# First stage in another order: modulation first, all of v among the filters

## The chip, the cores and the metric

The kernel runs on one core of a Trainium2 chip. The metric is the device time of one execution in microseconds (us). Each execution does the whole step in one launch. The engines of the core are TensorE (PE, with its weight loads PEld), VectorE (DVE), ScalarE (ACT), GpSimd (POOL) and SyncE (SP), which here only issues transfers. Each engine works through its own list of instructions in order and waits where an operand or a buffer is not ready.

## The reference

One inference step of a layer with D = 1024 on T = 640 tokens: 128 of a prompt and 512 of a sample, with separate conditioning vectors (c_ctx and c). Cut to what matters here:

```python
mod = (silu(cond) @ ada_w + ada_b).reshape(6, 1024)      # shift1 scale1 gate1 shift2 scale2 gate2
h = x * (1 + scale1) + shift1
q, f_fwd, f_bwd, i_raw, g_raw, hy, mg = split(h @ w_in)   # w_in: 1024 x 10240
# filters: three sine layers of 64, then @ filt_w4, times a window; to the frequency domain
# HGRN2 mixer: gates from f, v = i_raw, chunkwise scan per head and direction
# Hyena mixer: short conv, long conv through the frequency domain with the filters
mix = (sigmoid(mga) * (o_a @ proj_a) + sigmoid(mgb) * (o_b @ proj_b)) @ w_out
x = layer_norm(ALPHA * x + gate1 * mix)
x = layer_norm(ALPHA * x + gate2 * ((silu(gt) * up) @ ffn_w_out))   # gt, up from h2 @ ffn_w_in
```

Outputs are both token groups and the final scan states of the prompt.

## The kernel before, in words

All products are fp32. A product is made as three passes of rounded parts: high by high, high by low, low by high. The transposed input is held as hTh and hTl, four tiles each of 128 x 2 x 640. Each weight tile (512 KB, named raw) is loaded by SP, cast to its high part wh by ACT (L357 before) and its low part wl is made by a subtraction, on DVE or POOL (L181 is the helper tt that records all such operations). A table HIE says which engine casts, WSUB which one subtracts for the first units, LOOK how far ahead a unit's weights are asked for.

The program's stages: a first stage (function start), Winograd products M1 of several column groups of w_in, the long convolution, proj_b, the HGRN heads, w_out, the FFN and the output. The first stage runs over the tokens of the table PLAN:

- x0..x4 load the five token blocks, T0..T4 transpose them on PE into xT; p, t, q load and transpose small parameters; mlp is the filter MLP with its three sine layers.
- k0..k2 load the cosine/sine table and split it (kth, ktl).
- L0..L3 load a quarter of the filters' last weight (w4) and its window (win); A0..A3 make the windowed filter (matmuls ks; the results af, abh, abl), B0..B3 transform it (matmuls kp and k, 54 of 256 columns; sums and differences go to tiles ko); W0..W3 store ko to DRAM (kd) by the queue of ACT.
- D0..D3 load two 1 MB halves each of a block of ada_w into a ring of three buffers (tag araw), M0..M3 multiply them with the conditioning vectors (matmuls ada), copy the result (md), transpose it (adaT) and add it up into modT.
- h0..h7 scale and shift one eighth of xT with modT and split it into hTh and hTl.
- V0, V1 make a quarter of v each: two weight tiles, 120 matmuls of 256 columns, copies by ACT (L709), one store to vd by SP (L710). Before, the other two quarters are the tokens v2 and v3 of HGSEQ, the table of the HGRN stage, between g0/e0 and a1.
- e0 and e2 make the operands of the Winograd products (mb, then m5, m7, m6, m4, high and low) on DVE and ACT from hTh and hTl. The first of them closes the pool se, in whose memory the ring araw lies, and puts its tiles there. g, w and the digits load and split weights of M1 and run its products (L668). Q and Z are later blocks of ada_w, whose halves go through a buffer of tag v.

The tokens set the priority of the instructions; a scheduler then gives each engine its list, and the pools of buffers decide what must wait for what. In HGSEQ, a and b are the projections f of a head in both directions, q and g those of q and g, e the elementwise work of a head (Ln, scans, exponentials, products t), s its scan matmuls, that begin with transpositions kT.

```python
v = (vp if p < 2 else hg["p"]).tile([P, NB, 256], F32, tag="v", bufs=1 + p // 2, name=f"v{p}")
ada_load(*divmod(i, 2), vp, "v", 1)          # ada_next: the later ada blocks
close_se(); mo["y"], mo["close_t"] = pool("mtp")   # first call of m1_operands
```

Of the kernel before, what the change touches and what calls it, by code (L numbers as in the profile page):

```python
# [1784 lines left out]
```

## Time and profile before

| | |
|---|---|
| median of 3 runs | 1434.0 us (1432.09 to 1435.02) |
| profiled execution | 1434.2 us, its span 1431.9 us |
| PE busy | 1381.0 us, 96% of the span |
| DVE, ACT, POOL busy | 992.3, 617.3, 64.1 us |
| DMA | 195.64 MB, mean 137 GB/s |

The span reaches from the first to the last instruction. A matmul's record is longer than the distance to the next one, because matmuls overlap; what a matmul costs is read from the distance of their starts. A row of the waits says which instruction waited, for which, how long in all, how often and how long at most. A wait for several things is put down to the one that came last.

### The profile page before, as it was taken

To read this page: it belongs to the slowest core of one execution; us is meant where nothing else is said; L and a number is where in the kernel's file an instruction comes from. 1 tells how busy PE (TensorE), PEld (TensorE's weight loads), DVE (VectorE), ACT (ScalarE), POOL (GpSimd) and SP (SyncE) were. 2 spreads that over 40 slices of the span, in tenths; PEclk is the share of its full clock that TensorE was granted. 3 is DMA by queue.
4 is the path that set the end of the run, shared out by engine and by line. 5 is a ranking of instruction groups with operands and counts; after the bars stand their busy time and mean duration, and the time that the engine had idled before them with its cause. 6 is when DMAs were issued, how large, how long until landed. Compare 5 with 4: busy or idle time off the path is not lost. (4 is left out here: it accounts for less than half of the span.)

```text
span 1431.9 us, 23453 instructions
## 1 busy us (share of the span) xinstructions
PE 1381.0 (96%) x9513; PEld 1293.4 (90%) x9513; DVE 992.3 (69%) x1751; ACT 617.3 (43%) x1011; POOL 64.1 (4%) x56
## 2 busy tenths in 40 slices
PE   4999999999999999999999999999999999999997
PEld 2689889999999989999999999988999898898886
DVE  6886786647889734568788875579976665756426
ACT  3555554433323212455665673337543443442121
POOL 4230000020000000000000000000000000000003
PEclk9999999999999999999999999999999999999999
DMA  7944665674333374422232224632343323357211
GB/s 247 324 141 141 217 216 175 208 244 154 90 100 102 105 230 151 145 74 86 70 95 63 67 67 148 224 103 84 111 119 100 113 82 116 91 182 272 74 60 74
DMA packets 198856, 195.64 MB, mean 137 GB/s; under 512 B 7581, under 2 KB 155773, under 8 KB 197980
## 3 DMA queue, kind: packets, MB, share of 16 engines
q1 hardware_dynamic: 194860, 179.75, 39.9%
q0 software_dynamic: 2160, 9.15, 1.7%
q10 hardware_dynamic: 1728, 5.24, 0.9%
q8 instruction: 74, 1.21, 0.4%
q14 instruction: 34, 0.28, 0.1%
HBM read 162.91 MB, written 31.21 MB: 136 GB/s over the span
## 5 line engine op out<-in xcount | busy, mean ns | idle before, releaser
L181 DVE TENSOR_TENSOR wl<-raw,wh 128x1024 fp32r<-128x1024 f32 x96 | 117.3, 1224 | 134.8 <-ACT wh L357 131.2
L357 ACT CAST wh<-raw 128x1024 fp32r<-128x1024 f32 x90 | 94.1, 1049 | 221.8 <-PE pb L611 41.0
L1423 PE MATMUL fo<-wh,act 128*128 128x512 f32 (+1 forms) x440 | 130.7, 380 | 0.0
L1423 PEld LDWEIGHTS fo<-wh,act 128*128 128x128 f32 x440 | 81.2, 188 | 15.9
L1423 PE MATMUL fo<-wl,act 128*128 128x512 f32 (+1 forms) x220 | 83.4, 379 | 0.0
L611 PE MATMUL hy<-hTh,wh 128*128 128x320 f32 x256 | 79.6, 311 | 0.0
L611 PE MATMUL hy<-hTh,wl 128*128 128x320 f32 x256 | 79.2, 309 | 0.0
L611 PE MATMUL hy<-hTl,wh 128*128 128x320 f32 x256 | 79.1, 309 | 0.0
L611 PE MATMUL f<-hTh,wh 128*128 128x320 f32 x224 | 70.7, 316 | 0.0
L611 PE MATMUL f<-hTl,wh 128*128 128x320 f32 x224 | 69.7, 311 | 0.0
L611 PE MATMUL f<-hTh,wl 128*128 128x320 f32 x224 | 69.2, 309 | 0.0
L181 POOL TENSOR_TENSOR y<-y,gb 128x512 f32<-128x512 f32 x8 | 11.6, 1454 | 908.8 <-ACT y L170 908.5
L1423 PEld LDWEIGHTS fo<-wl,act 128*128 128x128 f32 x220 | 41.3, 188 | 7.9
L611 PEld LDWEIGHTS hy<-hTh,wh 128*128 128x128 f32 x256 | 48.1, 188 | 0.0
L611 PEld LDWEIGHTS hy<-hTl,wh 128*128 128x128 f32 x256 | 48.1, 188 | 0.0
L611 PEld LDWEIGHTS hy<-hTh,wl 128*128 128x128 f32 x256 | 48.1, 188 | 0.0
L707 PE MATMUL v<-wl,hTh 128*128 128x256 f32 x160 | 45.4, 287 | 1.6 <-DVE wl L181 1.6
L170 ACT ACT_TABLE_LOAD x36 | 46.2, 1283 | 1.4 <-PEq L1769 0.7
L707 PE MATMUL v<-wh,hTl 128*128 128x256 f32 x160 | 45.4, 286 | 0.1
L707 PE MATMUL v<-wh,hTh 128*128 128x256 f32 x160 | 45.1, 286 | 0.0
L611 PEld LDWEIGHTS f<-hTl,wh 128*128 128x128 f32 x224 | 42.2, 188 | 0.0
L611 PEld LDWEIGHTS f<-hTh,wh 128*128 128x128 f32 x224 | 42.1, 188 | 0.0
(2291 smaller groups left out, 4708.1 us busy)
## 6 DMA issues: line engine op xcount, KB each, us to landing
raw<-in_w_in SPq DMA_DIRECT2D x52, 512.0 KB, 4.0
rf<-in_ffn_w_in SPq DMA_DIRECT2D x42, 512.0 KB, 4.3
araw<-in_ada_w SPq DMA_DIRECT2D x20, 1024.0 KB, 5.8
rm<-in_w_in SPq DMA_DIRECT2D x28, 512.0 KB, 4.8
raw<-in_ffn_w_out SPq DMA_DIRECT2D x22, 512.0 KB, 5.0
sd<-my SPq DMA_DIRECT2D x28, 320.0 KB, 2.3
kk<-kd SPq DMA_DIRECT2D x20, 256.0 KB, 2.7
ad<-y SPq DMA_DIRECT2D x16, 320.0 KB, 4.4
```

The costliest lines, as they stand in the source:

```text
L170: r = S.activation(out, in_, func, bias=bias, scale=scale)
L181: return (eng or V).tensor_tensor(out=out, in0=a, in1=b, op=op)
L357: (V.tensor_copy if HIE[i] == "V" else S.copy)(hi, raw)
L611: r = PE.matmul(ps[:, 0:HT], w[a][:, k, :], x[b][:, k, c0:c0 + HT], start=k == 0 and i == 0, stop=k == kt - 1 and i == 2)
L707: PE.matmul(ps[:, (t - t0) * 256:(t - t0) * 256 + 256], hT[b][:, k, t * P:t * P + P], w[a][:, k % 4, :], start=k == 0 and i == 0, stop=k = ...
L1423: PE.matmul(ps, x(t, b, k0 + kk), w[a][:, kk, :], start=first and kk == 0 and i == 0, stop=last and kk == nk - 1 and i == 2)
```

## The change

PLAN is in another order. The loads of ada_w, of x and the modulation M0 to M3 and all of h come ahead of the second filter; then the filters and the four quarters of v alternate: L1 B0 V0 A1 W0 L2 B1 V1 A2 W1 L3 B2 V2 A3 W2 q B3 e0 g0 W3 V3. A new token c transposes the two conditioning vectors from a tile of their own (crow), which two DMAs of ACT's queue load, and makes their sigmoid ahead of the MLP; before, they were part of prow2 and of token t. v2 and v3 leave HGSEQ, and all four quarters use one buffer. The results ko of a filter leave from the ring araw (and kop from the ring xs of the pool se), before from buffers of the weight stream or from a tile of their own. All scaling of h goes to ACT (HMOD), all splits of the first stage's weights to DVE (WSUB).

```diff
-PLAN = """x0 k0 L0 k1 x4 k2 p mlp t L1 T0 x3 T4 A0 x2 D0 T2 A1 x1 L2 B0 M0 T1 D2 A2 M2 T3 h0 L3 B1 D1 A3 h1 B2 M1 D3 h2 h3 M3 h4 W2 W0 h5 h6 h7 W1 q V0 e0 B3 g0 W3 V1 m w0 e2 10 20 g1 ...
-HMOD = "SVSSVSSS"
+PLAN = """c mlp p x0 L0 x1 D0 x2 t k0 T0 T1 k1 D2 T2 x3 x4 k2 M0 D1 A0 T3 T4 M2 D3 M1 M3 h0 h1 h2 h3 h4 h5 h6 h7 L1 B0 V0 A1 W0 L2 B1 V1 A2 W1 L3 B2 V2 A3 W2 q B3 e0 g0 W3 V3 m w0 e2 10 20 g1 ...
+HMOD = "SSSSSSSS"
-WSUB = "VGGVVGGG"
+WSUB = "VVVVVVVVVVVV"
-HGSEQ = """a0 b0 q0 g0 e0 v2 v3 a1 b1 ...
+HGSEQ = """a0 b0 q0 g0 e0 a1 b1 ...
...
+    crow = sp.tile([16, P], F32, name="crow")
+    S.dma_start(crow[0:8], I["c_ctx"].rearrange("(k p) -> k p", p=P))
+    S.dma_start(crow[8:16], I["c"].rearrange("o (k p) -> (o k) p", p=P))
...
+    def cond_T():
+        ps = tr_bank("pr2_ps")
+        PE.transpose(ps[:, 0:16], crow, ident[0:16, 0:16])
+        V.tensor_copy(cT.rearrange("p a k -> p (a k)"), ps[:, 0:16])
         act(csig, cT, AF.Sigmoid)
...
-            if cc < 2:
-                t = wp.tile([P, n, 2, 256], F32, tag=("wh", "wl")[cc], bufs=HL_BUFS, name=f"ko{cc}_{nm}")
-            else:
-                t = sp.tile([P, n, 2, 256], F32, tag="ko", bufs=1, name=f"ko{cc}_{nm}")
+        ko = se.tile([P, 2, 2, 2, 256], F32, tag="araw", bufs=3, name=f"ko{cc}")
...
-        t = kout(1, "p")
+        t = se.tile([P, 1, 2, 256], F32, tag="xs", bufs=3, name=f"kop{cc}")
...
-            v = (vp if p < 2 else hg["p"]).tile([P, NB, 256], F32, tag="v", bufs=1 + p // 2, name=f"v{p}")
+            v = vp.tile([P, NB, 256], F32, tag="v", bufs=1, name=f"v{p}")
...
-        stream["stop"] = 4
+        stream["stop"] = 8
```

HIE and LOOK get four entries more at their head (S and 2), for the four weight tiles that V2 and V3 add to the first stage.

Three places show how instructions move. First SP's queue in the first stage, before (araw are halves of ada_w, w and win a filter's loads, raw the weights of V0 and V1):

```order
L397 DMA araw_0_318<-in_ada_w 128x4x512
L397 DMA araw_1_320<-in_ada_w 128x4x512
L450 DMA xs_393<-in_x_sample 128x1024
L523 DMA w_2_395<-in_filt_w 64x2x256 x2
L526 DMA win_398<-in_win 128x5x256
L397 DMA araw_0_505<-in_ada_w 128x4x512
L397 DMA araw_1_507<-in_ada_w 128x4x512
L523 DMA w_3_606<-in_filt_w 64x2x256 x2
L526 DMA win_609<-in_win 128x5x256
L397 DMA araw_0_682<-in_ada_w 128x4x512
...
L349 DMA raw_917<-in_w_in 128x4x256
```

The same queue after the change:

```order
L402 DMA araw_0_257<-in_ada_w 128x4x512
L402 DMA araw_1_259<-in_ada_w 128x4x512
L455 DMA xs_275<-in_x_sample 128x1024
L455 DMA xs_277<-in_x_sample 128x1024
L520 DMA kt_279<-in_kt 128x768
L402 DMA araw_0_303<-in_ada_w 128x4x512
L402 DMA araw_1_305<-in_ada_w 128x4x512
L402 DMA araw_0_412<-in_ada_w 128x4x512
L402 DMA araw_1_414<-in_ada_w 128x4x512
L528 DMA w_1_496<-in_filt_w 64x2x256 x2
L531 DMA win_499<-in_win 128x5x256
L354 DMA raw_571<-in_w_in 128x4x256
```

All eight halves of ada_w now stand ahead of the second filter's loads and of the first weight of v.

Second, DVE where the operands of M1 are made. Before, they begin ahead of the third filter's last sums (ko_1_815) and run on between the sums of the fourth (ko_0_1132):

```order
L181 TENSOR_TENSOR mb_0_1077<-hTh_872,hTl_873 128x640
L181 TENSOR_TENSOR ko_1_815<-k_1_1_788,ev_1_813 128x512
...
L181 TENSOR_TENSOR mb_0_1078<-mb_0_1078,mb_0_1075 128x640
L181 TENSOR_TENSOR m5l<-mb_0_1075,m5h 128x640
L181 TENSOR_TENSOR m7l<-mb_0_1076,m7h 128x640
...
L181 TENSOR_TENSOR ko_0_1132<-k_0_1_1105,ev_0_1130 128x512
...
L181 TENSOR_TENSOR m5l<-mb_2_1341,m5h 128x640
L181 TENSOR_TENSOR mb_2_1344<-mb_2_1344,mb_2_1341 128x640
L181 TENSOR_TENSOR ko_1_1163<-k_1_1_1136,ev_1_1161 128x512
```

After, they stand behind the fourth filter's last sum (ko_1343 is its tile):

```order
L181 TENSOR_TENSOR ko_1343<-k_1_1_1384,ev_1_1409 128x512
L181 TENSOR_TENSOR ko_1343<-ev_1_1409,k_1_1_1384 128x512
L181 TENSOR_TENSOR wma0l<-rm_0_1598,wma0h 128x512
L181 TENSOR_TENSOR mb_0_1425<-hTh_456,hTl_457 128x640
L181 TENSOR_TENSOR mb_0_1426<-hTh_456,hTl_457 128x640
...
L181 TENSOR_TENSOR m5l<-mb_0_1425,m5h 128x640
...
L181 TENSOR_TENSOR wmu0l<-rm_0_1598,wmu0h 128x1024
...
L181 TENSOR_TENSOR m5l<-mb_2_1620,m5h 128x640
...
L181 TENSOR_TENSOR m6l<-mb_2_1623,m6h 128x640
L181 TENSOR_TENSOR wmg1l<-rm_1_1671,wmg1h 128x1024
```

On PE the products that use them follow the last quarter of v (v_4_1561); ada_1903 is the fifth block of ada_w:

```order
L707 MATMUL v_4_1561<-wh_1456,hTl_487 128x256
L707 MATMUL v_4_1561<-wl_1457,hTh_486 128x256
L668 MATMUL ma_1640<-hTh_456,wmg0h 128x320
...
L668 MATMUL mc_1677<-m5h,wmu0h 128x320
L668 MATMUL mc_1677<-m5l,wmu0h 128x320
L668 MATMUL ma_1640<-m6h,wms0h 128x320
...
L411 MATMUL ada_1903<-araw_0_1589,scT 32x512 x4
...
L411 MATMUL ada_1903<-araw_1_1908,scT 32x512
L668 MATMUL ma_1690<-hTh_456,wmg1l 128x320
```

So the operands are now made while the last quarter of v and the first products run, and no longer beside two quarters of v and a filter.

Third, DVE in the HGRN stage, where v2 and v3 were. Before:

```order
L181 TENSOR_TENSOR t_0_6148<-t_0_6148,q_6083 128x1280
L181 TENSOR_TENSOR t_0_6149<-t_0_6149,sg_6080 128x1280
L181 TENSOR_TENSOR t_0_6146<-t_0_6146,sg_6080 128x1280
L181 TENSOR_TENSOR t_0_6147<-t_0_6148,ff_6068 128x640
L181 TENSOR_TENSOR t_0_6150<-t_0_6146,gg_6072 128x640
L181 TENSOR_TENSOR t_0_6151<-t_0_6146,xx_6076 128x320
L181 TENSOR_TENSOR wl_6319<-raw_6316,wh_6318 128x1024
```

After:

```order
L181 TENSOR_TENSOR t_0_6427<-t_0_6427,q_6362 128x1280
L181 TENSOR_TENSOR wl_6523<-raw_6520,wh_6522 128x1024
L181 TENSOR_TENSOR t_0_6428<-t_0_6428,sg_6359 128x1280
L181 TENSOR_TENSOR t_0_6425<-t_0_6425,sg_6359 128x1280
L181 TENSOR_TENSOR t_0_6426<-t_0_6427,ff_6347 128x640
L181 TENSOR_TENSOR t_0_6429<-t_0_6425,gg_6351 128x640
```

A split of a weight now stands between the products with q and sg; on PE the transposition kT of t_0_6429 follows both units of f.

More of the change, by code (lines that the diff above doesn't have):

```diff
@@ L133 @@
 WPRI = 2
-HIE = """SSSSVVSVSVSSSSSSSVVVSVVSVSSVSSSSSSSSSSSSSSSSSSSSSSSSSSSSSSSSSSSSSSSSSSSSSSSSSSSSSSSSSSSSSSSSSSSSSSSSSSSSSSSSSS"""
-LOOK = """22222012202102201120122111222222222222222222222222222222222222222222222222222222222222222222222222222222222222"""
+HIE = """SSSSSSSSVVSVSVSSSSSSSVVVSVVSVSSVSSSSSSSSSSSSSSSSSSSSSSSSSSSSSSSSSSSSSSSSSSSSSSSSSSSSSSSSSSSSSSSSSSSSSSSSSSSSSS"""
+LOOK = """222222222012202102201120122111222222222222222222222222222222222222222222222222222222222222222222222222222222222222"""
 CONVSEQ = """a0 b0 c0 d0 e0 a1 b1 c1 f0 d1 e1 a2 b2 f1 s04 c2 s00 d2 x0 p0 s01 e2 i00 s02 a3 i01 s03 b3 i02 i03 f2 o00 c3 d3 e3 o01 a4 f3 s14 x1 s10 b4 c4 p1 s11 d4 i10 s12 e4 a5 i11 s13 b5 c5 d5 i12 f4 i13 o10 e5 a6 o11 f5 b6 s24 x2 s20 p2 s21 c6 i20 d6 s22 e6 i21 s23 a7 b7 i22 i23 c7 o20 f6 d7 o21 m0 e7 f7 s34 s30 n0 x3 m1 p3 s31 i30 s32 i31 s33 n1 i32 i33 o30 o31"""
-HGSEQ = """a0 b0 q0 g0 e0 v2 v3 a1 b1 q1 g1 s0 e1 a2 b2 q2 g2 s1 e2 a3 b3 q3 g3 s2 e3 a4 b4 q4 g4 s3 e4 a5 b5 q5 g5 s4 e5 a6 b6 q6 g6 s5 e6 a7 b7 q7 g7 s6 e7 s7 c m0 m1 t m2 m3 p0 m4 p1 m5 p2 m6 p3 m7 p4 p5 p6 p7"""
+HGSEQ = """a0 b0 q0 g0 e0 a1 b1 q1 g1 s0 e1 a2 b2 q2 g2 s1 e2 a3 b3 q3 g3 s2 e3 a4 b4 q4 g4 s3 e4 a5 b5 q5 g5 s4 e5 a6 b6 q6 g6 s5 e6 a7 b7 q7 g7 s6 e7 s7 c m0 m1 t m2 m3 p0 m4 p1 m5 p2 m6 p3 m7 p4 p5 p6 p7"""
 PHB = 2
@@ L287, in body @@
     prow1 = sp.tile([P, P], F32, name="prow1")
-    prow2 = sp.tile([65, P], F32, name="prow2")
+    prow2 = sp.tile([49, P], F32, name="prow2")
+    crow = sp.tile([16, P], F32, name="crow")
+    S.dma_start(crow[0:8], I["c_ctx"].rearrange("(k p) -> k p", p=P))
+    S.dma_start(crow[8:16], I["c"].rearrange("o (k p) -> (o k) p", p=P))
     skp_all = sp.tile([1, D], F32, name="skp_all")
     def params_load():
-        G.dma_start(prow2[49:57], I["c_ctx"].rearrange("(k p) -> k p", p=P))
-        G.dma_start(prow2[57:65], I["c"].rearrange("o (k p) -> (o k) p", p=P))
         G.dma_start(skp_all, I["hy_skip"])
@@ L312, in params_T @@
             tt(scT[:, :, a:a + 1].rearrange("p k a -> p a k"), cT[:, a:a + 1, :], csig[:, a:a + 1, :], ALU.mult)
+    def params_T():
+        ps = tr_bank("pr3_ps")
+        PE.transpose(ps[:, 0:49], prow2, ident[0:49, 0:49])
         V.tensor_copy(prT2, ps[:, 0:49])
@@ L561, in kern_b @@
         kth_ = (kth, ktl)
-        def kout(n, nm):
-            if cc < 2:
-                t = wp.tile([P, n, 2, 256], F32, tag=("wh", "wl")[cc], bufs=HL_BUFS, name=f"ko{cc}_{nm}")
-            else:
-                t = sp.tile([P, n, 2, 256], F32, tag="ko", bufs=1, name=f"ko{cc}_{nm}")
-            return t
+        ko = se.tile([P, 2, 2, 2, 256], F32, tag="araw", bufs=3, name=f"ko{cc}")
         pk = o_bank(f"kp{cc}")
@@ L589, in kern_b @@
             od = pk[1].rearrange("p (x n) -> p x n", x=2)
-            t = kout(2, kt)
+            t = ko[:, kt]
             tt(t[:, 0], od, ev, ALU.add)
@@ L715, in v_add @@
         U(v_unit(p), w_tm(w_in, 0, 4, COL_I + p * 256, 256), w_tm(w_in, 4, 4, COL_I + p * 256, 256))
-    v_add(0)
-    v_add(1)
+    for p in range(4):
+        v_add(p)
     vu = units[:]
@@ L763, in step @@
             else:
-                dict(p=params_load, t=params_T, q=params)[op]()
+                dict(p=params_load, c=cond_T, t=params_T, q=params)[op]()
         for tok in PLAN.split():
```

6 lines of the change are left out of this document (1 added, 5 removed).

## The prediction

> **What bounds the kernel now.** I read the page's busy shares first, then the windows stage by stage, then PE's and SP's waits in the first stage, and last the timeline around the places where the changed order moves something.
>
> ```profile
> span 1431.9 us, 23453 instructions
> PE 1381.0 (96%) x9513; PEld 1293.4 (90%) x9513; DVE 992.3 (69%) x1751; ACT 617.3 (43%) x1011; POOL 64.1 (4%) x56
> ```
>
> PE is busy for 96% of the span, and the change leaves PE's work as it is (it only moves it). So the question is the 51 us in which PE stands still. The windows (columns: PE, PEld, DVE, ACT, POOL busy with their counts, granted clock, DMA share, GB/s) say where they lie:
>
> ```profile
> 0.00:20.00 20.00, 5.57 (x20) 2.63 (x21) 8.42 (x25) 4.51 (x7) 11.81 (x22) 1.00 0.76 211
> 20.00:40.00 20.00, 15.84 (x72) 9.68 (x71) 16.82 (x39) 10.97 (x26) 5.11 (x3) 0.83 0.88 310
> 40.00:60.00 20.00, 18.48 (x133) 13.55 (x132) 18.39 (x37) 11.19 (x24) 7.89 (x5) 1.00 0.81 281
> 60.00:80.00 20.00, 17.10 (x125) 12.83 (x123) 14.33 (x28) 13.14 (x22) 9.28 (x5) 1.00 0.88 300
> 80.00:100.00 20.00, 19.71 (x150) 19.52 (x151) 19.58 (x35) 12.71 (x22) 5.67 (x3) 0.91 0.28 107
> 575.00:600.00 25.00, 24.32 (x198) 24.12 (x197) 15.04 (x20) 11.45 (x16) 0.00 (x0) 1.00 0.37 117
> 1050.00:1275.00 225.00, 212.18 (x1392) 204.47 (x1391) 148.58 (x249) 92.82 (x168) 0.00 (x0) 1.00 0.35 105
> ```
>
> In the first 100 us PE idles 14.4 + 4.2 + 1.5 + 2.9 + 0.3 = 23.3 us; the 12.8 us of 1050:1275 are the FFN's, which the change does not touch. What PE and SP wait for in the first 125 us:
>
> ```profile
> PE f L506 <- ACT sa L170: 7.2, 1, 7.2
> PE pr_ps L276 <- DMA frow<-in_filt_b: 4.7, 1, 4.7
> PE k L585 <- DVE af L181: 2.1, 1, 2.1
> PE mc L668 <- DVE wmu0l L181: 0.3, 1, 0.3
> ...
> SPq L526 <- DVE af L181: 19.1, 2, 10.2
> ```
>
> The first two, 11.9 us, are the start of the program and the chain of sines of the filter MLP, which the change keeps. The last row is SP standing behind the third and fourth window of the filters, with the ada loads and the weights of v behind it.
>
> **First stage: when can v begin?** Before, SP reaches the last ada loads and the first v weights here:
>
> ```profile
> 48.46 10.54 SPq L397 DMA_DIRECT2D araw<-in_ada_w  x4
> 59.09 3.70 SPq L349 DMA_DIRECT2D raw<-in_w_in  x3
> ...
> L707 PE MATMUL v<-wh,hTh x80: 280/283/415, 71.5 to 116.3; 128*128 128x256 f32 x80
> ```
>
> v's first matmul starts at 71.5 us. Now the loads of the last two filters come behind V0's in SP's queue, so SP is no longer held at windows; the ring of three 1 MB buffers holds it instead, and the weights of V0 stand behind the eighth ada load. Two bounds on V0's start. From below, by bytes, with the tiles' shapes in the code: ahead of the second V0 weight stand x (5 x 0.5 MB), the table (3 x 0.38), eight ada loads (8 x 1.05), two sets of filter columns and windows (2 x 0.9) and two weights (2 x 0.5), some 15 MB.
>
> ```profile
> 20.00:28.00 8.00, 6.62 (x30) 4.43 (x28) 7.99 (x24) 6.07 (x17) 2.78 (x2) 1.00 1.03 377
> 28.00:36.00 8.00, 5.21 (x15) 2.64 (x16) 7.27 (x11) 3.42 (x7) 2.33 (x2) 0.61 0.66 211
> ```
>
> By 20 us 211 x 20 = 4.2 MB have moved; the other 10.8 MB at the 377 GB/s of the best slice take 29 us and land at 49, at the 310 of 20:40 they take 35 and land at 55. Behind the landing come a cast and a split, 2.3 us, so 51 to 57:
>
> ```profile
> L181 DVE TENSOR_TENSOR wl<-raw,wh 128x1024 fp32r<-128x1024 f32 x96 | 117.3, 1224 | 134.8 <-ACT wh L357 131.2
> L357 ACT CAST wh<-raw 128x1024 fp32r<-128x1024 f32 x90 | 94.1, 1049 | 221.8 <-PE pb L611 41.0
> ```
>
> From above, by the ring: the eighth load is issued when the fifth, whose buffer it takes, has been read, and each turn costs a landing and PE's reading:
>
> ```profile
> araw<-in_ada_w SPq DMA_DIRECT2D x9, 1024.0 KB, 8.5
> ```
>
> Following PE's order (M0 behind the transposes at about 27, ada2 behind A0, ada1 behind B0 at about 45) I put the eighth issue at 45, its landing at 45 + 8.5 = 53.5; then its quads, the copy of md, four transposes and the last h (about 4 us) give 58, and 62 if a turn slips by 4. I take **58**, nearer to the ring, because the ring's row is of this stage and is not a best slice.
>
> From V0's start on PE is bound by its own work, since weights and filters now arrive ahead: V0, B1, V1, A2, B2, V2, A3, B3, V3 are 480 matmuls of v, 162 of B and 20 of A. The spacing of 256 columns is that of v2 and v3, of which every third is in the first row here (237 steps in 29.4 us less the 0.7 us of idle time in 575:600, so 0.121); the last two rows are of 512 columns:
>
> ```profile
> L707 PE MATMUL v<-wh,hTh x80: 280/283/284, 566.9 to 596.3; 128*128 128x256 f32 x80
> ...
> 65.72 0.40 PE L543 MATMUL ks<-whl,hf_hi 128*128 128x512 f32 x1
> 65.95 0.40 PE L544 MATMUL ks<-whl,hf_lo 128*128 128x512 f32 x1
> ```
>
> (480 + 162) x 0.12 + 20 x 0.235 = 81.7 us: the Winograd products (M1) start at 58 + 81.7 = 139.7. Before they start at 116.6 (row below); v2 and v3, which have moved ahead of them, are 240 x 0.12 = 28.8 us, so 145.4 is what to compare. **First stage: -5.7 us** (V0 at 51: -12.7; at 62: -1.7).
>
> **M1's start.** Before, the operands of M1 (e0, e2) are made on DVE beside V0, B3 and V1, and M1 starts without a stop: of its waits only the 0.3 us quoted above. After, they stand on DVE behind the sums of B3 (ko), and only V3 is left to cover them. Call X the end of B3 on PE. Ahead of X + 1.6 (two pairs of sums) DVE cannot begin; up to wmg1l it then has 23 operations of 640 columns, 7 of 512, 2 of 1024 and one of 320:
>
> ```profile
> L181 DVE TENSOR_TENSOR mb<-mb,mb 128x640 f32<-128x640 f32 x8 | 6.5, 815 | 0.0
> L181 DVE TENSOR_TENSOR rm<-rm 128x512 f32<-128x512 f32 x2 | 1.4, 692 | 0.1
> ```
>
> 23 x 0.82 + 7 x 0.69 + 2 x 1.22 + 0.5 = 26.6 us, some 2 less because neighbours overlap (580.72 and 581.46 below, 0.74 apart), so wmg1l at about X + 27 with ACT's casts of m5 to m4 between. Against that stands PE's work ahead of its first use: 82 matmuls of V3 (9.8 us) and 56 products of 320 columns at 0.147 (8.2 us, the row stands at HGRN) and five ada matmuls (0.6 us), 18.6 us. Stall 8.4 us. The second ada column meets the same time: its load waits until V3 has been stored, since both use one buffer.
>
> ```profile
> L668 PE MATMUL ma<-hTh,wmg0h x4: 309/309/312, 116.6 to 118.0; 128*128 128x320 f32 x4
> ...
> 121.41 0.45 SPq L397 DMA_DIRECT2D araw<-in_ada_w  x1
> ...
> araw<-in_ada_w SPq DMA_DIRECT2D x20, 1024.0 KB, 5.8
> ```
>
> From M1's start to that load 4.8 us, then 5.8 to land, read, and the second half 5.8 again: X + 9.8 + 16.4 = X + 26, and on SP two weights of M1 stand behind that load. Two chains with one answer; I take **+8.4**, with 5 (casts early, loads short) to 12 (both slip by one landing of 3 to 4 us) as ends. A stop also costs clock. After the 2.1 us wait for af quoted above, which ended at 80.15, matmuls stood further apart:
>
> ```profile
> 80.96 0.40 PE L585 MATMUL k<-abh,kth 128*128 128x256 f32 x1
> 81.16 0.41 PE L585 MATMUL k<-abl,kth 128*128 128x256 f32 x1
> ...
> 84.14 0.39 PE L707 MATMUL v<-wl,hTh 128*128 128x256 f32 x1
> ```
>
> 0.21 us in place of 0.12 over 3.2 us is a loss of 1.4 us; the long stall here is broken by single products, so I add **+1.0** (0 to 1.5).
>
> The Trainium skill says it too: "TensorE: Matmul & The Clock Gate", Part 1 on the HAM clock gate, has the array at half rate after an idle window of about 3.4 us and for about 3.4 us of work, with windows that run freely. The row of 28:36, with its granted clock of 0.61 and 2.8 us of idle time, agrees; by the page's figures each such stop would lose 1.7 us in place of my 1.4.
>
> **HGRN.** Before, v2 and v3 stand between g of head 0 and f of head 1 and cover DVE's and ACT's work for head 0:
>
> ```profile
> 576.53 1.47 DVE L181 TENSOR_TENSOR t<-t,q 128x1280 f32<-128x1280 f32 x1
> 577.92 2.88 DVE L181 TENSOR_TENSOR t<-t,sg 128x1280 f32<-128x1280 f32 x2
> 580.72 0.82 DVE L181 TENSOR_TENSOR t<-t,ff 128x640 f32<-128x640 f32 x1
> 581.46 0.82 DVE L181 TENSOR_TENSOR t<-t,gg 128x640 f32<-128x640 f32 x1
> ...
> 596.67 0.31 PE L611 MATMUL f<-hTh,wh 128*128 128x320 f32 x1
> 598.14 0.31 PE L611 MATMUL f<-hTl,wh 128*128 128x320 f32 x1
> ```
>
> The last two rows, ten matmuls apart, give 0.147 for 320 columns. In these times: PE would now begin f at 566.9 and finish its two units (96 products) at 580.9; the next row on PE is the transposition kT of t*gg. On DVE a weight's split (1.22) now stands between t*q and t*sg, so t*gg ends at 582.3 + 1.2 = 583.5. Stall 2.6 us; the 0.7 us of idle time that 575:600 has before goes: **+1.9** (0 if the split falls elsewhere, 4 if ACT's cast for it slips behind the second exponential).
>
> **Edits at nothing.** cond_T and its sigmoid move ahead of the MLP, beside the 7.2 us wait for its sines. The splits that leave POOL cost DVE 1.22 us each, beside V units in which DVE has no more than a filter's products; without that cover it is 12 x 1.22 us. The scaling of h, all on ACT, is in the 4 us above. ko in the ring of the ada buffers: the stores to kd have a V unit's 14.4 us (120 matmuls) to leave ahead of the next filter; its price is in M1's start, where operands take that memory.
>
> **Sum.** -5.7 + 8.4 + 1.0 + 1.9 = +5.6. The profiled execution took 1434.2 us, 1431.9 of it span; the median shown is 1434.0, so nothing is to be corrected: 1434.2 + 5.6 = **1440 us**.
>
> **The rivals.** (a) Faster: DMA keeps to its best rate and V0 starts at 51 (-12.7), while DVE's operands slip between the sums of B3 so that M1's stall is 5 with no slow clock after it, and HGRN hides its own (0): -7.7, 1426.5; with only the first half of this it is about 1432. For it: the ring frees loads as early as PE reads, and the clock is at 1.00 in 40:60. Against: 211 GB/s in 28:36 shows that this stage does not keep its rate where buffers hold loads. It decides if V0 starts ahead of 51. (b) The moved v only changes places: early gain and M1's stall cancel (-5.7 + 5 + 1): 1434.5. For it: both of M1's chains have slack of a few us in my working. (c) Worse: the ring slips, V0 at 62 (-1.7), M1's stall 12 + 1.5, HGRN 4: +15.8, 1450. For it: M1's loads stand behind one another in SP's queue and each slip of one delays all. (d) No gain ahead and no stall behind, because the scheduler's order was made by its own estimate of durations; the order of PE's rows, where M1's first products are broken into pairs, speaks against.
>
> **How the numbers follow.** A measurement of this kernel tells about 0.2% (2.9 us) from no change. Forecast (1437 to 1446) 0.44, (a) 0.21, (b) and (d) 0.20, (c) 0.15. Faster by over 0.2% is most of (a): 0.21; within 0.2%: (b), (d): 0.20; slower: the forecast and (c): 0.59. The range leaves out half of (a)'s far end and the tail of (c): 1428 to 1450; the forecast's own range is 1437 to 1446.
>
> **What would show it.** V0's first matmul (L707) at 58 (51 to 62); L668's first at 140 (133 to 144); between it and 20 us later PE idle of 8 us, named by DVE's m5l, m6l, wmg1l or by araw; a wait of kT for t*gg of 2 to 3 us in HGRN; the rest shifted, not changed. If V0 starts ahead of 51, or PE's windows behind M1's start show less than 3 us idle, the prediction is wrong, and on the fast side.

## The result and the profile after

The changed kernel takes 1450.8 us (median, 1450.05 to 1451.53) against 1434.1 us of the kernel before on the same chip: a ratio of 1.0127, interval 1.0115 to 1.0139. It is slower by 16.7 us, where 5.6 were forecast; 1450.8 is 0.8 us above the range, and the direction is the one that had the most chance. The head of the page of the profiled execution:

```profile
span 1449.8 us, 23479 instructions
PE 1383.3 (95%) x9514; PEld 1296.3 (89%) x9514; DVE 996.1 (69%) x1752; ACT 620.0 (43%) x1015; POOL 48.1 (3%) x49
```

PE's busy time grew by 2.3 us and the span by 17.9, so most of the loss is PE standing still. (The two profiled executions differ by 17.9 us, the medians by 16.7.) Four marks on PE divide the program: the first matmul of v, the first product of M1 (L668 with wmg0h), the first product hy of the long convolution, and, in the HGRN stage, the way from the first g to the first proj_a product (pa). The columns are us; "comparable" takes v2 and v3 (28.8 us) into account, as the prediction did.

| | before | forecast | after | after less before |
|---|---|---|---|---|
| v starts | 71.5 | 58 | 61.3 | |
| M1 starts (before: comparable) | 145.4 | 139.7 | 150.3 | +4.9 (forecast -5.7) |
| M1's start to the first hy | 193.2 | +9.4 | 204.0 | +10.8 |
| first g to first pa (before without v2, v3) | 270.2 | +1.9 | 272.0 | +1.8 |
| the rest of the span | | 0 | | +0.4 |

The first two marks and the one behind M1 are in the groups by tile:

```profile
L707 PE MATMUL v<-wh,hTh x160: 277/283/384, 61.3 to 149.9; 128*128 128x256 f32 x160
...
L668 PE MATMUL ma<-hTh,wmg0h x4: 309/309/312, 150.3 to 151.6; 128*128 128x320 f32 x4
...
L611 PE MATMUL hy<-hTh,wh x256: 303/309/394, 354.3 to 512.2; 128*128 128x320 f32 x128
```

**The first stage.** The windows of the changed kernel, with the columns of the windows in the prediction:

```profile
20.00:40.00 20.00, 12.21 (x77) 7.39 (x70) 13.60 (x29) 9.28 (x23) 6.43 (x4) 0.84 1.01 380
40.00:48.00 8.00, 7.23 (x57) 6.05 (x56) 1.36 (x2) 8.00 (x17) 3.41 (x2) 0.98 0.15 33
48.00:56.00 8.00, 4.98 (x41) 2.32 (x39) 4.50 (x12) 3.11 (x7) 0.00 (x0) 1.00 0.96 321
56.00:62.00 6.00, 5.26 (x20) 4.25 (x21) 5.07 (x13) 3.65 (x6) 0.00 (x0) 0.72 1.06 385
61.30:150.30 89.00, 84.34 (x665) 81.51 (x665) 52.15 (x81) 36.09 (x58) 14.29 (x10) 1.00 0.43 137
```

Three readings. From 20 to 40 us the transfers run at 380 GB/s and PE has little to do (7.8 us idle, 4.2 before); from 40 to 48 it is the other way round, 33 GB/s, since SP stands in the ring until 46.7; and from 48 on, at 321 and 385 GB/s, the transfers catch up, V0's weights among them. Behind v's start PE idles 4.7 us of 89. What SP waited for in the first 130 us of the same kernel (in all, times, longest):

```profile
SPq L402 <- DMA araw<-in_ada_w: 15.2, 4, 6.0
SPq L402 <- PE ada L411: 11.4, 4, 7.9
...
SPq L354 <- DMA kd<-kop: 5.2, 1, 5.2
```

(The last row is the third weight of v, issued at 57.40: it stood behind the store of a filter's result. The second, issued at 51.76, had waited 2.4 us for an ada load to land.) Then the timeline (start and length; in brackets the idle time ahead and what ended it) of SP, ACT and PE around v's start:

```profile
23.57 23.15 SPq L402 DMA_DIRECT2D araw<-in_ada_w  x4
...
48.72 9.05 SPq L354 DMA_DIRECT2D raw<-in_w_in  x3
...
53.51 2.24 ACTq L598 DMA_DIRECT2D kd<-ko  x2
55.79 0.58 ACT L422 COPY md<-ada 128x512 f32<-128x512 f32 x1 [1.72 <-DVE ko L181]
...
58.32 1.04 ACT L362 CAST wh<-raw 128x1024 fp32r<-128x1024 f32 x1 [1.15 <-DMA raw<-in_w_in]
...
51.05 1.92 PE L411 MATMUL ada<-araw,scT 128*32 128x512 f32 x16
56.43 0.66 PE L435 MATMUL adaT<-cst,md 128*128 128x128 f32 x4 [3.45 <-ACT md L422]
57.39 0.75 PE L548 MATMUL ks<-whl,hf_hi 128*128 128x512 f32 x1 [0.30 <-DVE whl L181]
```

The last block of the modulation was summed on PE at 53.0 (51.05 + 1.92), but its copy md stands in ACT's list behind the store of the first filter's results, which waits for DVE's last ko. The weight of V0, asked for at 48.72, is cast at 58.32. Then the transposition, ten filter products at half rate (0.43 us apart, the clock was at 0.72), and v at 61.3. So three things end within a few us of each other: the modulation, the weight and the filter's products. PE's waits behind v's start:

```profile
PE v L707 <- POOL hTl L181: 1.8, 2, 1.1
...
PE kp L572 <- POOL abl L181: 1.3, 2, 0.7
PE k L585 <- POOL abl L181: 1.0, 2, 0.5
```

Of PE's 4.7 us of idle time behind v's start 4.1 go by name to POOL's low parts of h (hTl) and of the filters (abl).

**M1.** The 20 us behind M1's start, the changed kernel first:

```profile
150.30:170.30 20.00, 12.89 (x67) 9.38 (x66) 19.67 (x27) 11.79 (x18) 0.00 (x0) 0.91 0.58 191
```

and the kernel before at its own start of M1:

```profile
116.60:136.60 20.00, 19.72 (x131) 18.96 (x130) 13.98 (x20) 11.10 (x19) 0.00 (x0) 1.00 0.52 171
```

DVE is busy for 19.7 of 20 us and PE idles 7.1 where it idled 0.3. PE's waits in 150 to 175 us name ACT most of all:

```profile
PE ma L668 <- ACT wmg2h L619: 3.4, 1, 3.4
PE mc L668 <- ACT wmu0h L619: 1.6, 1, 1.6
PE ada L411 <- DMA araw<-in_ada_w: 0.9, 1, 0.9
PE ma L668 <- DVE m6l L181: 0.8, 1, 0.8
```

The timeline of DVE and SP says whose time it is:

```profile
144.90 3.03 DVE L181 TENSOR_TENSOR mb<-hTh,hTl 128x640 f32<-128x640 f32 x4
...
156.25 1.22 DVE L181 TENSOR_TENSOR wmu0l<-rm,wmu0h 128x1024 fp32r<-128x1024 f32 x1
...
157.50 2.95 SPq L633 DMA_DIRECT2D rm<-in_w_in  x2
```

The load of the third weight (rm, whose cast wmg2h PE waits for at the longest) is issued at 157.50, as DVE's split wmu0l of the buffer before it ends (156.25 + 1.22): ACT's name stands there, DVE's list decides. DVE began the operands at 144.9, 5.4 us ahead of M1's start; before, at 87.4, 29.2 us ahead.

**HGRN.** In the timeline of DVE and PE at head 0, PE waits for the product with gg, with a weight's split ahead of the two with sg. Before, PE had no such wait at head 0, only 0.7 us in v for a split; a wait of kT of 1.4 us at a later head stands in both kernels.

```profile
622.35 1.22 DVE L181 TENSOR_TENSOR wl<-raw,wh 128x1024 fp32r<-128x1024 f32 x1
623.49 2.88 DVE L181 TENSOR_TENSOR t<-t,sg 128x1280 f32<-128x1280 f32 x2
...
627.02 0.81 DVE L181 TENSOR_TENSOR t<-t,gg 128x640 f32<-128x640 f32 x1
...
627.89 0.55 PE L1232 MATMUL kT<-cst,t 128*128 128x128 f32 x3 [2.26 <-DVE t L181]
```

### The profile page after: what moved, and what is told of

Its sections match the earlier page's. It is cut to its first block, busy times and chain, and to the rows that moved or that the text cites. A ratio compares the mean times of both kernels' runs of the same rounds, so it can differ in the third digit from the quotient of the medians.

```text
span 1449.8 us, 23479 instructions
## 1 busy us (share of the span) xinstructions
PE 1383.3 (95%) x9514; PEld 1296.3 (89%) x9514; DVE 996.1 (69%) x1752; ACT 620.0 (43%) x1015; POOL 48.1 (3%) x49
## 5 line engine op out<-in xcount | busy, mean ns | idle before, releaser
L181 DVE TENSOR_TENSOR wl<-raw,wh 128x1024 fp32r<-128x1024 f32 x101 | 123.4, 1224 | 127.2 <-ACT wh L362 126.1
L611 PEld LDWEIGHTS f<-hTh,wl 128*128 128x128 f32 x224 | 42.1, 188 | 0.0
```

The costliest lines, as they stand in the source:

```text
L181: return (eng or V).tensor_tensor(out=out, in0=a, in1=b, op=op)
L611: r = PE.matmul(ps[:, 0:HT], w[a][:, k, :], x[b][:, k, c0:c0 + HT], start=k == 0 and i == 0, stop=k == kt - 1 and i == 2)
```

## The experiments

The theory after the result: M1 loses because its operands have lost their lead on DVE; the first stage loses because PE has too little to do ahead of v and because POOL's parts, which were costed at nothing, now stand in PE's way. The rivals: M1 is held by SP's queue (the ada blocks and the store of v ahead of its weights), and the first stage by the bytes and the ring. Every edit is on the changed kernel unless "before" is said. The marks of all runs stand here; ratios are to the kernel before on the same chip, with their intervals. "M1 starts" of a kernel that has v2, v3 or one of them in the HGRN stage is given with 28.8 or 14.4 us added, and its HGRN with as much taken off.

| | v starts | M1 starts | M1 to hy | HGRN | median, us | ratio |
|---|---|---|---|---|---|---|
| before | 71.5 | 145.4 | 193.2 | 270.2 | 1434.1 | 1 |
| after | 61.3 | 150.3 | 204.0 | 272.0 | 1450.8 | 1.0127 |
| e1 operands ahead of B3 | 61.8 | 151.2 | 199.7 | 273.6 | 1447.8 | 1.0106 (1.0082 to 1.0130) |
| e2 md on DVE | 62.3 | 151.6 | 203.9 | 273.4 | 1451.8 | 1.0131 (1.0105 to 1.0156) |
| e3 before, only v moved | 69.8 | 144.9 | 196.8 | 272.0 | 1441.6 | 1.0059 (1.0039 to 1.0080) |
| e4 POOL's parts to DVE | 61.2 | 146.5 | 204.2 | 272.0 | 1446.6 | 1.0095 (1.0074 to 1.0116) |
| e5 operands two quarters early | 61.1 | 148.7 | 193.9 | 272.0 | 1440.9 | 1.0057 (1.0037 to 1.0076) |
| e6 HGRN's split to POOL | 62.6 | 152.1 | 204.9 | 273.2 | 1454.7 | 1.0140 (1.0111 to 1.0168) |
| e7 half the ada loads | 53.1 | 147.0 | 203.1 | 272.1 | 1446.2 | 1.0091 (1.0071 to 1.0110) |
| e8 e4 + e5 + e6 | 61.2 | 146.2 | 195.4 | 274.7 | 1439.1 | 1.0040 (1.0025 to 1.0056) |
| e9 e4 + e5 | 60.7 | 145.2 | 194.4 | 273.5 | 1436.7 | 1.0022 (1.0011 to 1.0032) |
| e10 before, splits off POOL | 71.1 | 143.0 | 194.1 | 270.3 | 1431.5 | 0.9987 (0.9976 to 0.9999) |
| e12 e9, filler ahead of v | 59.6 | 142.2 | 197.9 | 273.6 | 1435.0 | 1.0007 (0.9995 to 1.0018) |
| e13 e12, one quarter in HGRN | 58.7 | 141.4 | 208.6 | 269.3 | 1444.7 | 1.0086 (1.0074 to 1.0099) |
| e14 e12, ada loads by POOL | 59.6 | 142.9 | 209.7 | 273.6 | 1448.8 | 1.0108 (1.0093 to 1.0123) |
| e15 after, ada loads by POOL | 62.5 | 151.5 | 215.2 | 272.0 | 1463.4 | 1.0213 (1.0196 to 1.0230) |
| e17 e10, ada loads by POOL | 72.9 | 144.8 | 208.3 | 270.3 | 1446.0 | 1.0092 (1.0074 to 1.0111) |

The part from the first product of w_out to the first of the FFN's second weight (tile fo), which no edit touches, took 351.8 to 358.7 us in these profiles (355.8 before, 356.6 after). A total that moves by a few us says nothing of an edit, then; the marks of its stage do.

**The lead of M1's operands: e1 and e5.** e1 has the first operands ahead of the fourth filter, which needs its results ko to leave from a tile of their own, since the operands take the ring's memory:

```diff
-... W2 q B3 e0 g0 W3 V3 m w0 e2 10 ...
+... W2 q e0 B3 g0 W3 V3 m w0 e2 10 ...
-        ko = se.tile([P, 2, 2, 2, 256], F32, tag="araw", bufs=3, name=f"ko{cc}")
+        if cc < 3:
+            ko = se.tile([P, 2, 2, 2, 256], F32, tag="araw", bufs=3, name=f"ko{cc}")
...
+            t = ko[:, kt] if cc < 3 else sp.tile([P, 2, 2, 256], F32, tag="ko", bufs=1, name=f"ko{cc}_{kt}")
```

> The changed kernel, with one thing moved: the operands e0 come ahead of B3 again, and for that the fourth filter's sums leave from a tile of their own (as all of the kernel before's last two did). Theory A (M1's operands behind B3 have too little cover, worth 10.8 us): the idle time of PE in the 25 us behind M1's start goes from 7 to under 2 us and the slow clock there goes with it, the time falls by 7 to 10 us, to 1441 to 1444. Rival B (M1 waits for the fifth ada block and the weights behind it on SP, which the store of V3 holds): operands are no longer named in the waits, but ada and wmg2h are, and the time falls by less than 3 us.

Measured: M1 199.7 us instead of 204.0, so 6.5 of the 10.8 us lost are still there; the total falls by 3.0 us. Neither theory fits whole: 4.3 us come back, and the waits that are left name wmu0h (2.3 us) and DVE's wmg1l (1.5), and neither ada nor wmg2h. The operands begin at 136.3, a lead of 14.9 us, but the last of them at 151.2, behind M1's start:

```profile
L181 DVE TENSOR_TENSOR mb<-hTh,hTl x8: 810/818/1884, 136.3 to 151.2; 128x640 f32<-128x640 f32 x8
```

e5 has the same tiles and moves both operand tokens further: e0 two quarters of v ahead of M1, e2 one, with V2 itself behind A3:

```diff
-... B2 V2 A3 W2 q B3 e0 g0 W3 V3 m w0 e2 10 ...
+... B2 A3 W2 q e0 V2 B3 g0 W3 e2 V3 m w0 10 ...
```

> The changed kernel, with the third filter's first half and M1's operands moved further ahead: A3 W2 e0 V2 B3 W3 e2 V3, and the fourth filter's sums in a tile of their own. The trace of the kernel with e0 just ahead of B3 has DVE begin the operands 15 us before M1 and lose 6.5 us from M1's start to the first unit of hy, where the changed kernel begins 5.4 us before and loses 10.8 and the kernel before 29 us before and loses nothing. Theory A (lead of DVE's operands decides): lead 29 us or more, loss in M1 under 3 us, time 1450.8 - 8 to 10 = 1441 to 1443. Rival B (the rest is due to SP, where weights of M1 stand behind an ada load that waits for the store of V3): loss stays at 4 to 6.5 us, waits named wmg2h, wmu or ada; time 1444 to 1447.

Measured: M1 takes 193.9 us, 0.7 more than before, and the total falls by 10 us. All the first sums of the operands end ahead of M1's start (148.7), as the groups show:

```profile
L181 DVE TENSOR_TENSOR mb<-hTh,hTl x8: 812/822/1933, 125.7 to 141.4; 128x640 f32<-128x640 f32 x8
...
L672 PE MATMUL ma<-hTh,wmg0h x4: 309/309/312, 148.7 to 150.1; 128*128 128x320 f32 x4
```

and PE's waits in 140 to 170 us are down to one:

```profile
PE mc L672 <- ACT wmu0h L623: 1.3, 1, 1.3
```

By lead, from the first mb to M1's start, the loss in M1 goes 29.2 us: 0 (before), 23.0: 0.7 (e5), 18.2: 1.2 (e9) and 2.2 (e8), 14.9: 6.5 (e1), 5.4: 10.8 (after), 5.9: 11.0 (e4). So M1's loss in the changed kernel is the operands' lead, and nearly all of it comes back with SP's order as it was: in e5 the store of v (150.14), the fifth ada block (153.14) and M1's next weights (155.25) follow one another as in the changed kernel. Three versions stand outside this row, e3, e12 and e13; the next part comes back to them.

**What POOL does: e4 and e6.** e4 gives the low parts of h (HSUB) and of the filters (ASUB) to DVE throughout:

```diff
-HSUB = "GVVVVGVG"
+HSUB = "VVVVVVVV"
-ASUB = "GVVVGVGVGGGGVGVGVVVG"
+ASUB = "VVVVVVVVVVVVVVVVVVVV"
```

> The changed kernel, with POOL's subtractions of the first stage (hTl and abl) all on DVE. Theory A (PE's waits for POOL in the first stage are lost time, 1.8 + 1.3 + 1.0 us): they go, and the time falls by 3 to 4 us. Rival B (DVE is then late in their place): the waits take DVE's names and the time stays within 1 us or rises.

Measured: from v's start to M1's 85.3 us instead of 89.0, M1 as late as it was. PE's idle time in this stretch falls from 4.7 to 1.3 us (the window of e4):

```profile
61.20:146.50 85.30, 84.04 (x665) 81.46 (x664) 54.05 (x91) 36.07 (x58) 0.00 (x0) 1.00 0.46 145
```

So 3.7 us of the first stage's error are POOL's work, which the prediction had at nothing. e6 goes the other way in HGRN and gives the split that stands between DVE's products, and every 39th one, to POOL:

```diff
-WSUB = "VVVVVVVVVVVV"
+WSUB = "V" * 38 + "G"
```

> The changed kernel, with the one weight split that stands between t*q and t*sg of head 0 on POOL in place of DVE. Theory A (that split, 1.2 us on DVE, delays t*gg and with it kT): the wait of kT falls from its value by about 1.2 us; time -1 to -1.5 us. Rival B (the exponentials on ACT, with the weight's cast between them, set it): no change of the wait; time within 0.5 us.

Measured: kT waits longer, not shorter (3.4 us at the longest instead of 2.3). The split ran beside DVE's two products with sg, and these took 4.92 us instead of 2.88, the first 3.51 and the second, when the split had ended, 1.48 (timeline of POOL and DVE):

```profile
624.10 3.29 POOL L181 TENSOR_TENSOR wl<-raw,wh 128x1024 fp32r<-128x1024 f32 x1 [72.40 <-ACT wh L362]
625.23 4.92 DVE L181 TENSOR_TENSOR t<-t,sg 128x1280 f32<-128x1280 f32 x2
```

So the split's 1.22 us on DVE is the cheaper place, and HGRN's loss was left as it is.

**Ahead of v: e2, e7 and e12.** e2 copies the modulation's sums on DVE, off ACT's list:

```diff
-        S.copy(md, ada["ps"].pop(nb))
+        (V.tensor_copy if nb < 4 else S.copy)(md, ada["ps"].pop(nb))
```

> The changed kernel, with the copies md of the four modulation blocks on DVE in place of ACT. Theory A (the chain of the modulation is late because md stands behind the filter's casts on ACT, a wait of 4.4 us on PE at 37): the transposition adaT of block 2 comes 4 us earlier, the ring of ada buffers turns earlier, V0 starts at 57 to 59 in place of 61.3, the time falls by 2 to 4 us. Rival B (the ring's landings set it): adaT is earlier, but ada of blocks 1 and 3 is not, V0 starts within 1 us of 61.3 and the time stays within 1 us.

Measured: nothing gained; v starts at 62.3. PE's wait has only got another name, because on DVE the copy stands behind the same last ko:

```profile
PE adaT L435 <- DVE md L422: 10.3, 3, 6.7
```

e7 leaves out the loads of the second and fourth block of ada_w and uses the third's in their place, so it makes all products but not the reference's modulation:

```diff
-                    ada_load(i, n, se, "araw", 3)
+                    if i in (1, 3):
+                        ada["raw"][i, n] = ada["two"][n]
+                    else: ...
```

> The changed kernel, leaving out the ada loads of blocks 1 and 3 (4 MB); their products read block 2's tiles, so the modulation is not the reference's; all products are made. Theory A (the ring of three buffers and the bytes hold SP until 46.8 us and so V0): SP reaches V0's weights ahead of 30 us, V0 starts at 47 to 53 in place of 61.3, time -8 to -14 us (1437 to 1443). Rival B (the chain through md, adaT and h on ACT and DVE sets V0): V0 at 56 or later, time -1 to -5 us.

Measured: SP asks for V0's first weight at 28.26 instead of 48.72 and v starts at 53.1, 8.2 us earlier, but M1 only 3.3: the second filter's products, which PE did ahead of v before, now come behind it. Ring and bytes, which this edit takes away together, hold v's start; of its gain less than half reaches M1, and the total falls by 4.6 us where 8 to 14 were expected. What is worth time is what PE can do in the meantime, which e12 tries: to e9 it adds another front, with the second filter's products (A1) and its transform (B1) ahead of v.

```diff
-... k2 M0 D1 A0 T3 T4 M2 D3 M1 M3 h0 ... h7 L1 B0 V0 A1 W0 L2 B1 V1 A2 W1 L3 ...
+... k2 M0 L1 D1 A0 T3 T4 M2 D3 B0 A1 M1 B1 M3 h0 ... h7 V0 W0 L2 V1 A2 W1 L3 ...
```

> The two repairs, and the second filter ahead of the last modulation blocks again: M0 L1 D1 A0 T3 T4 M2 D3 B0 A1 M1 B1 M3 h V0. Theory A (the changed order left PE without other work while the eight ada loads pass the ring, so 25 us of idle time stand ahead of V0 where B1 and A1 could run): V0 starts at 58 to 62 as before, but B1's 6.4 us lie ahead of it or beside it; M1 starts 4 to 7 us earlier than in the kernel with two repairs (146), time 1437 - 4 to 7 = 1430 to 1433. Rival B (L1's loads ahead of D1 hold the ring and the modulation by as much): V0 starts at 64 or later, time 1436 to 1439.

Measured: M1 starts at 142.2, 3.2 us ahead of the kernel before. M1 itself takes 197.9, so 3.5 of the gain over e9 are given back there. The total is that of the kernel before (1.0007, 0.9995 to 1.0018), where 1430 to 1433 was expected.

**The parts alone and together: e3, e8, e9, e10, e13.** e3 is the kernel before with v2 and v3 moved behind V1, the one buffer for v and the tables' entries for their four weights, and nothing else in the front:

```diff
-... V0 e0 B3 g0 W3 V1 m w0 e2 ...
+... V0 e0 B3 g0 W3 V1 V2 V3 m w0 e2 ...
-HGSEQ = """a0 b0 q0 g0 e0 v2 v3 a1 b1 ...
+HGSEQ = """a0 b0 q0 g0 e0 a1 b1 ...
```

> The kernel before, with one part of the change alone: v2 and v3 leave the HGRN stage and follow V1 in the first stage; order, buffers of ko and all else as before. Theory A (the move of v itself costs nothing in the first stage and uncovers DVE in HGRN): M1's start moves by 28.8 us, no stall behind it, HGRN has a wait of kT for t*gg of 2 to 3 us; time 1434.1 + 1.9 = 1436 (1435 to 1437). Rival B (the longer lag before M1 lets DMA and DVE fill up work that now stalls elsewhere): 1431 to 1434. Rival C (the later vd store and the ada loads through one buffer stall M1 as in the changed kernel): 1440 and above.

Measured: M1 starts 0.5 us earlier (comparable), M1 loses 3.6 us, HGRN 1.8. By these marks moving v costs some 5 us by itself (the median is 8.2 above the kernel before, but 2.9 of that stand between w_out and fo, which the edit does not touch); the new front costs the first stage 5.4 and M1 7.2 more. M1's loss here is not the operands': they begin 59 us ahead, and 3.9 us of PE's waits in M1 name ACT's copies of sums (mu). e8 is e4, e5 and e6 together, e9 is e4 and e5.

> The changed kernel with three edits together: the early operands of the first run of this set, POOL's subtractions of the first stage on DVE, and the one split in HGRN on POOL. If the losses add up: -9 - 4 - 1 = 1437 (1434 to 1440). If DVE, which now carries POOL's part too, becomes late with the operands: 1441 and above.

> The changed kernel with two repairs, those that showed a gain by themselves: M1's operands early (e0 ahead of V2, fourth sums in a tile of their own; 10 us) and POOL's subtractions of the first stage on DVE (4 us). If both add up, 1450.8 - 14 = 1437 (1435 to 1439); V0 still starts at 61, M1 at 146, 195 from there to hy, as in the run that also had a split of HGRN on POOL, which cost 2 us there.

Measured: e9 is at a ratio of 1.0022, the changed kernel at 1.0127: the first stage is level with the kernel before (145.2 to 145.4), M1 loses 1.2, HGRN 3.3. e8 is at 1.0040, with an interval that overlaps e9's; its HGRN stage, which has the POOL split, is 1.2 us longer. That e9 loses 3.3 in HGRN and the changed kernel 1.8 is the clock: the wait of kT at head 0 is the same (2.27 and 2.26 us), but behind it the granted clock (last but two) fell in e9, while it stayed at 1.00 in the changed kernel:

```profile
614.00:616.00 2.00, 2.00 (x9) 2.00 (x8) 2.00 (x3) 0.00 (x1) 0.00 (x0) 0.51 0.00 0
616.00:618.00 2.00, 2.00 (x11) 2.00 (x11) 1.29 (x3) 0.00 (x0) 0.00 (x0) 0.64 0.44 126
```

e10 takes POOL's splits of the first weights out of the kernel before, one part of the change alone:

```diff
-WSUB = "VGGVVGGG"
+WSUB = "VVVVVVVV"
```

> The kernel before with one table of the change alone: the splits of the first eight weights all on DVE (WSUB). Its trace has two splits of 2.7 us on POOL at 72.7, a wait of DVE for abl behind them (3.5 us) and of PE for that (2.1 us). Theory A (these splits cost PE 2 us and a slow clock): 1433.5 - 2 to 3 = 1431. Rival B (DVE is full in that stage and late elsewhere in its place): within 1 us of 1433.5, or slower.

Measured: 0.9987 (0.9976 to 0.9999), M1 2.4 us earlier. In 60 to 80 us, where PE was busy for 17.10 us before, the window of e10 has:

```profile
60.00:80.00 20.00, 19.05 (x143) 14.98 (x142) 17.14 (x34) 14.03 (x24) 4.19 (x4) 1.00 0.90 302
```

This is the only version faster than both, and by as little as its interval can tell. e13 is e12 with the last quarter of v back behind e0 in HGRN:

```diff
-HGSEQ = """a0 b0 q0 g0 e0 a1 b1 ...
+HGSEQ = """a0 b0 q0 g0 e0 v3 a1 b1 ...
```

> The kernel with the second filter ahead, and the last quarter of v left in HGRN between e0 and a1, as half of it was in the kernel before. Theory A (14.4 us of v cover head 0's elementwise work, 2.3 us of stall, and its absence ahead of M1 takes cover away there): HGRN's wait of kT goes from 3.7 to 1.4 us or less (-2.3), M1's part loses 2 to 6 us because its operands now have B3 and V2 alone; time +0 to +4 against the kernel with the second filter ahead. Rival B (operands that begin ahead of V2 are done in time): M1 loses nothing, time -2.

Measured: HGRN 269.3, even 0.9 below the kernel before and 4.3 below e12: the wait at head 0 (2.3 us) and the slow clock behind it are gone, so v does cover this work. But M1 loses 15.4 us: without V3 ahead of it, its operands have a lead of 5.0 us, as in the changed kernel, and 4.6 us of PE's waits name the fourth filter's sums (ko) besides. The total is 9.7 us above e12, more than either theory allowed.

**SP's queue: e14, e15, e17.** The rival for M1: the later ada blocks stand in SP's queue behind the store of v and ahead of M1's weights. The edit puts those loads on POOL's queue, in e12 (e14), in the changed kernel (e15) and in e10 (e17):

```diff
-        ada_load(*divmod(i, 2), vp, "v", 1)
+        ada_load(*divmod(i, 2), vp, "v", 1, eng=G)
```

> The kernel with two repairs and the second filter ahead, with the later ada blocks' loads (those that wait for the store of V3 and then for one another) on POOL's queue in place of SP's. Its trace has M1 start 3.0 us earlier than without the filter ahead and loses 3.5 of it again, with ACT waiting for weights of M1 (wmg2h, wma1h) that SP issued behind an ada load. Theory A (SP's queue order behind the vd store is the second cause of M1's loss): the 197.9 us from M1's start to hy go to 193 to 195, time 1435.0 - 3 to 5 = 1430 to 1432. Rival B (DMA's own rate sets the landing of those weights): 197 to 198 again, time within 1 us.

> The changed kernel with this alone. Theory A (operands on DVE are the main cause, SP's order the second): the wait for wmg2h (3.4 us) goes, but DVE's operands end as late, m5l, m6l and wmg1l are named in its place; loss in M1 10.8 to 8 to 10; time 1450.8 - 1 to 3. Rival B (SP's order is as large a cause as the operands): loss 5 to 7, time -4 to -6.

> The kernel before with the first eight splits on DVE (1431.5 us) and the later ada loads on POOL's queue. In its trace M1 has next to no waits, so both theories expect no more than 1 us: 1430.5 to 1432; slower if POOL's issuing disturbs DVE.

Measured: M1 is longer in all three, by 11.8 (e14 over e12), 11.2 (e15 over the changed kernel) and 14.2 us (e17 over e10); no theory had expected a loss of that size. A load itself takes little longer (median 5.8 us to landing in M1 of e14, 5.3 in e12). PE's longest wait in M1's first 60 us of e14, 3.6 us, names one of M1's own sums (DVE's mu), and DVE's list says where it stood. First e12, then e14:

```profile
185.59 0.48 DVE L181 TENSOR_TENSOR mu<-mc,mu 128x320 f32<-128x320 f32 x1
191.20 0.69 DVE L181 TENSOR_TENSOR wma4l<-rm,wma4h 128x512 fp32r<-128x512 f32 x1 [5.12 <-ACT wma4h L623]
```

```profile
192.18 0.69 DVE L181 TENSOR_TENSOR wma4l<-rm,wma4h 128x512 fp32r<-128x512 f32 x1 [4.73 <-ACT wma4h L623]
192.79 0.49 DVE L181 TENSOR_TENSOR mu<-mc,mu 128x320 f32<-128x320 f32 x1
```

In both the split wma4l comes only when its late weight has been cast; in e12 the sum stands ahead of it, in e14 behind it. So the edit moved more than a queue: the scheduler gave DVE another list. The same happens near M1's end in all three: a sum that PE needs stands behind two casts of weights (wh from raw) on DVE, the first of which waits 4.4 (e14), 4.7 (e15) and 4.9 us (e17) for its load, and PE waits 4.1, 3.1 and 4.2 us for the sum. In the kernels that they were made from, this cast waits for nothing and the sum stands ahead of the second. These three runs therefore do not test SP's order by itself, and how much of the 11 to 14 us is the queue and how much the lists is open. That SP's order is not needed for M1's loss rests on e5.

## Why the prediction was wrong, step by step

**The step that failed** is the first stage: "From V0's start on PE is bound by its own work, since weights and filters now arrive ahead", with 81.7 us, and v's start at 58 ahead of it. Forecast -5.7, measured +4.9: 10.6 of the 12.3 us by which the marks of the profiled execution (17.9) exceed the sum (5.6).

- *From v's start to M1's*: 89.0 us instead of 81.7, 7.3 of the error. Weights and filters did arrive, but their low parts did not: 4.1 us of waits name POOL's hTl and abl, and e4 gets 3.7 back by giving them to DVE. The prediction asked which splits leave POOL and not which stay: "edits at nothing" named HMOD and WSUB, while HSUB and ASUB, which the change leaves as they were, came to stand directly ahead of PE. Some 0.6 us are the spacing (0.121, not 0.120, over 642 matmuls); the other 3.0 are not assigned. (The scaling of h on ACT was not tested by itself; 0.5 us of waits name its hTh.)
- *v's start*: 61.3 instead of 58, 3.3 of the error, inside the range given (51 to 62). The eighth ada load was issued at 46.4 (45 forecast) and its sums were done at 53.0 (landing alone 53.5 forecast): the ring was right. The step behind it was short: "about 4 us" from there to v were 8.3. md stood behind the store of ko in ACT's list, V0's weight was still coming, and the second filter's products stood ahead of v at half rate. e2 moved the copy off ACT's list and gained nothing, since on DVE it stood behind the same sum.
- *Byte bound*: the forecast took 310 GB/s for 20 to 40 us; it was 380, and then 33 from 40 to 48. The ring and the bytes are not two bounds of which one holds: the ring empties the queues and then the bytes are due all the same.

**M1's start.** Right in mechanism, and by 1.4 us in size: 10.8 against 8.4 + 1.0. The idle time was 6.8 us more than before in the first 20 us, under the forecast 8.4 and inside its 5 to 12; e5 and e1 show that it is the lead of the operands. The slow clock was the term sized too small: 1.0 forecast, and after one stop. In the 30 us from M1's start PE ran 122 matmuls instead of 198, 76 fewer or 11.2 us at 0.147; 6.8 of that is idle time, the other 4.4 are slower work. The windows with the granted clock (last but two) show it:

```profile
162.00:164.00 2.00, 1.60 (x10) 0.46 (x10) 2.00 (x4) 1.19 (x3) 0.00 (x0) 0.81 0.56 163
164.00:166.00 2.00, 2.00 (x10) 1.53 (x7) 2.00 (x4) 1.51 (x3) 0.00 (x0) 0.50 0.25 34
166.00:168.00 2.00, 1.17 (x6) 0.91 (x6) 2.00 (x4) 1.97 (x3) 0.00 (x0) 0.84 0.88 302
168.00:170.00 2.00, 1.08 (x6) 0.73 (x7) 2.00 (x3) 1.18 (x3) 0.00 (x0) 1.00 0.50 193
170.00:172.00 2.00, 2.00 (x4) 0.64 (x3) 1.97 (x3) 0.00 (x0) 0.00 (x0) 0.51 0.00 0
172.00:174.00 2.00, 2.00 (x11) 2.00 (x10) 1.51 (x3) 0.00 (x0) 0.00 (x0) 0.63 0.00 0
```

If the clock is either full or half, the half lasted 0.76 + 2.0 + 0.64 = 3.4 us in the first stretch and 1.96 + 1.48 = 3.4 in the second. Two stops, then, of up to 1.7 us each, where the prediction counted one; the last us of the 4.4 is not assigned. The names of the waits were as said for m6l and araw, but for the largest (wmg2h) it is the weight's buffer, freed late by DVE, and not the operand itself; the second ada column was there within 0.9 us.

The exceptions to the rule of the lead have other waits. e3 has a lead of 59 us and loses 3.6 in M1, e12 18.3 and loses 4.7 (e9, at the same lead, 1.2). No operand of e0 or e2 is named in either: PE waits for ACT's copies of sums (mu), 3.9 us in e3 and 2.5 in e12, against 0.3 in e9. In e12 one such copy (157.59) stands in ACT's list behind the cast wma1h, which waited 2.0 us for its weight. So there M1 is held by casts that stand ahead of its sums, and not by its operands; no run isolates what makes those weights late.

**HGRN.** +1.8 (1.9 forecast), the wait of kT 2.26 us (2.6 forecast) with the split where the prediction put it, and e13 shows the cover by its return. The mechanism is right; that the number is so near is in part luck. The prediction had no slow clock behind this stop, and in this execution none came; in e9, with the same stop, one did, and the stage took 1.5 us more.

**The rest**: 0 forecast, +0.4 measured. **The rivals.** (a) and (b) needed the earlier start of v to last until M1, and it did not. (c) gave 1450 with v at 62 (61.3), M1 13.5 (10.8) and HGRN 4 (1.8); its total is nearly the measured one, but by luck: it had a gain of 1.7 us in the first stage where 4.9 were lost, and a larger loss in M1 and HGRN than came. (d) fell with the idle windows of M1.

## What to carry to other kernels

When a change brings a consumer forward, list all that feeds it, also the operations that the change leaves alone, and ask of each in whose list it stands and behind what: here low parts left on the slow engine cost 3.7 us, and a copy queued behind a store was on the path too, though moving it alone gained nothing. Operands that a second engine makes need a lead about as long as that engine's work on them (here some 27 us by the prediction's count; with 23 M1 lost 0.7 us, with 18 it lost 1.2 to 2.2, with 15 it lost 6.5), counted in the first engine's work that stands between, and moving that work elsewhere takes the lead away. A wait's name is the last link only: here ACT's casts and the transfers were named, and DVE's list decided. And an edit of one queue can reorder the lists of other engines, so compare those lists before the queue is blamed.
